# A decoder block with a Strassen-Winograd down projection: block sum T1 split under the up projection, sums S4 and T4 made ahead of their casts, results parked in dead activation blocks

## The chip, the cores and the metric

The kernel runs on one core of one Trainium2 chip. The metric is the device time of one launch in microseconds. The profile is of one execution, taken by the hardware profiler; its engines are TensorE (PE, with PEld for the weight loads that overlap the matmuls), VectorE (DVE), ScalarE (ACT), GpSimd (POOL) and SyncE (SP), whose queue issues nearly all DMAs here.

## The reference

One decoder layer on 512 tokens of width 1024, in float32:

```python
h   = rms_norm(x, norm_mix)
q, k, v, u = split(h @ w_in)                 # 4 x 512 columns
a   = moba_attention(q, k, v)                # 8 heads x 64, ALiBi, blocks of 256, causal
p   = multiscale_pool(u, w_pool, pool_scale) # 4 groups x 128
x   = x + concat(a, p) @ w_out
h   = rms_norm(x, norm_mlp)
x   = x + square(relu(h @ w_up)) @ w_down    # w_up 1024 x 4096, w_down 4096 x 1024
out = rms_norm(x, norm_final)
```

The change touches the last product alone: `square(relu(...)) @ w_down`.

## The kernel before

**Precision.** Each float32 operand is split in two float32r parts: `split_into` (line 147) has ScalarE cast the high part and VectorE subtract it from the source for the low part. A product is then three matmuls (`mm3`, line 195): high by high, high by low, low by high.

**Up projection.** `h @ w_up` is made transposed, in 32 blocks `f` of 128 hidden units by 512 tokens, 24 matmuls each. The loop of line 768 takes a block's weights from `ready`, has `sqrelu` make relu (ScalarE) and square (VectorE), and splits one further weight block (`prefetch`).

**Down projection.** Hidden blocks 0 to 27 form 14 pairs. Of each pair, the 2 x 2 blocks of activations (token halves by hidden blocks) and of w_down (hidden blocks by column halves) are multiplied in the Winograd form of Strassen's method, 7 products in place of 8. The blocks of activations and their sums lie in `a_p[p]`, six slots of 256 tokens; `a_sums` makes three of the sums. Of the weights three sums are needed: T1, T2, T3 are made by `t_sums` under the up projection and stored to scratch in DRAM (`t_store`): T2 and T1 in `t21`, T3 in `t3`. T4 is made in sweep 0 by one addition to a raw block (line 754); S4, the fourth sum of activations, is made by the subtraction of line 730. The products run in two sweeps over the pairs, since a core has eight banks:

- sweep 0 (line 809): per pair m1, m6, m7, m4, 24 matmuls of 512 columns. `a_split` splits four slots of the next pair's activations. Two `advance` calls split two blocks of weights for later.
- between the sweeps m1, m6, m7 are combined and leave their banks to `y` and `y2` (lines 816 to 828), which take the buffers of the normed activations (pool `hp`).
- sweep 1 (line 839): per pair m2, m5, m3, 18 matmuls. `a_split` first makes S4 of the next pair and then splits three slots. Two `advance` calls split T1 (512 columns, loaded as float32 from `t21`) and the pair's second block (1024 columns); at pairs 3, 5, 7, 9 of the list of steps (`LAST_AT`) a third splits a block of the tail. Two additions of finished blocks into `x` follow (`add_y`), eight in all.

Hidden blocks 28 to 31 are multiplied plainly in the tail (line 870), into the same banks, followed by the residual, the final norm and the stores.

**Order.** The program fixes each engine's order as it is written (`in_program_order`). Buffers set the rest: four raw blocks and four split ones in rotation, two of split activations (`ah`, `al`), which `t_load` uses under the up projection. SP issues the loads in program order too, and waits there for the buffer of each.

Of the kernel before, what the change touches and what calls it, by code (L numbers as in the profile page):

```python
# [50 lines left out]
def hybrid_block(  # L51
# [67 lines left out]
    for sweep, p, k in steps:  # L119
        if sweep == 2:  # L120
            parts = [(slice(None), rows(2 * PAIRS + p))]
        elif (sweep, k) == (0, 0):
            parts = [(LEFT, rows(2 * p, LEFT)), (RIGHT, t21[p][:, LEFT])]
        elif (sweep, k) == (0, 1):
            parts = [(LEFT, rows(2 * p + 1, LEFT)), (RIGHT, t3[p])]
# [546 lines left out]
    a_p = [ap.tile([P, 6, HT], F32, tag=f"a{p}", name=f"a{p}") for p in range(PAIRS)]
    tsum = {}

    def t_load(p):
        r0 = sp.tile([P, D], F32, tag="ah", name="r0", bufs=2)
        r1 = sp.tile([P, T], F32, tag="al", name="r1", bufs=2, padded_shape=[P, D])
        nc.sync.dma_start(r0, rows(2 * p))
        nc.sync.dma_start(r1, rows(2 * p + 1, RIGHT))
# [18 lines left out]
    def sqrelu(f, acc, ks=(0, 1)):  # L698
# [40 lines left out]
    def advance():
        sweep, p, k = steps.pop(0)  # L740
        raw, shape = raws.pop(0)
        if sweep == 2:
# [15 lines left out]
        if (sweep, k) == (0, 0):
            t2_of.append(raw[:, RIGHT])
        if k == 1 or sweep:  # L760
            load()
        if (sweep, k) == (0, 1):
            load()

    t2_of, w_pair = [], []
# [158 lines left out]
```

## Time and profile before

| | us |
|---|---|
| median of 3 runs (lowest, highest) | 541.66 (541.39, 542.94) |
| the profiled execution | 543.16 |
| its span, first to last instruction | 541.4 |
| TensorE busy, of the span | 520.1 |
| VectorE busy | 378.9 |
| ScalarE busy | 247.5 |

A busy TensorE is not one at its peak, since matmuls overlap: the records are 0.39 us long and begin 0.23 us apart. So the starts are what to read: the distance of two starts is the pace, and a larger one is a loss. In the profile, names without their numbers stand for all buffers of a kind: `whi` and `wlo` are split weights, `ah` and `al` split activations, `a` is a slot of `a_p`, `t` a scratch tensor, `r` the blocks of which the sums are made, `z` the relu, `yh` and `yl` the tiles `y` and `y2`, `wl_h` and `wl_l` the tail's weights.

### The profile page before, as it was taken

The page shows a single profiled execution, that of the slowest core. Times are in us where ns is not written, and L with a number is a line of the kernel's source. Part 1 is how long each engine was busy: PE and PEld are TensorE (multiplying, and loading weights), DVE is VectorE, ACT ScalarE, POOL GpSimd, SP SyncE. Part 2 cuts the span into 40 slices and gives each one's busy share as a digit, 9 for nine tenths or more (in the row PEclk, how much of TensorE's full clock was granted, in tenths as well). Part 3 has the DMA queues.
Part 4 walks back from the last instruction along what each step waited for, and adds up shares of the span by engine and source line. Part 5 has one row for each costly group of instructions (what it writes and reads, how often), then busy time and mean ns, then how long its engine had stood idle before and what let it go on. Part 6 is the DMA issues. An engine that isn't in the chain of part 4 may idle for free.

```text
span 541.4 us, 6738 instructions
## 1 busy us (share of the span) xinstructions
PE 520.1 (96%) x2411; PEld 427.7 (79%) x2411; DVE 378.9 (70%) x619; ACT 247.5 (46%) x415; POOL 56.0 (10%) x59
## 2 busy tenths in 40 slices
PE   8999999997999999999999999999999998899995
PEld 5888878886888898888888888887888875576784
DVE  4764898888968658655765576657878778767653
ACT  4534586876635433323232323245555545455233
POOL 2330351615300100000000000000000000000002
PEclk9999999999999999999999999999999999999999
DMA  8441240303234137867867878624555444556013
GB/s 281 146 116 41 69 125 11 123 6 117 78 117 119 37 93 234 276 228 245 300 215 251 270 240 259 227 77 157 199 195 205 163 169 157 185 184 213 2 40 117
DMA packets 72037, 85.14 MB, mean 157 GB/s; under 512 B 4033, under 2 KB 49601, under 8 KB 72002
## 3 DMA queue, kind: packets, MB, share of 16 engines
q1 hardware_dynamic: 71424, 83.64, 46.9%
q10 hardware_dynamic: 578, 1.05, 0.5%
q8 instruction: 19, 0.31, 0.2%
q14 instruction: 16, 0.13, 0.1%
HBM read 71.57 MB, written 13.11 MB: 156 GB/s over the span
## 4 chain that ended last, share of the span: by engine, by line
PE 77%; DVE 10%; ACT 6%; issue 5%; DMA 1%; POOL 0%; SPq 0%; POOLq 0%; DVEq 0%; ACTq 0%
PE bank L199 23%; PE bank L197 23%; PE bank L198 23%; PE bank L297 3%; PE bank L430 2%; ACT whi L148 1%; ACT ah L148 1%; PE bank L219 1%; DMA wvr<-in_w_in_dram 1%; DVE al L149 1%; PE bank L459 1%; DVE wlo L149 1%; DVE ptl L465 1%; DVE wl_l L149 1%; DVE p L436 1%
## 5 line engine op out<-in xcount | busy, mean ns | idle before, releaser
L197 PE MATMUL bank<-hh,whi 128*128 128x512 f32 (+1 forms) x376 | 141.7, 377 | 0.2 <-DVE qs L392 0.2
L199 PE MATMUL bank<-hh,wlo 128*128 128x512 f32 (+1 forms) x376 | 141.2, 376 | 0.0
L198 PE MATMUL bank<-hl,whi 128*128 128x512 f32 (+1 forms) x376 | 141.2, 376 | 0.0
L149 DVE TENSOR_TENSOR wlo<-raw,whi 128x1024 fp32r<-128x1024 f32 x101 | 116.5, 1161 | 33.5 <-ACT whi L148 32.7
L148 ACT CAST whi<-raw 128x1024 fp32r<-128x1024 f32 (+1 forms) x104 | 102.0, 994 | 37.6 <-DVE raw L754 29.3
L197 PE MATMUL bank<-whi,ah 128*128 128x512 f32 x196 | 77.9, 398 | 5.7 <-ACT ah L148 5.1
L197 PEld LDWEIGHTS bank<-hh,whi 128*128 128x128 f32 x376 | 70.8, 188 | 13.3 <-PE bank L459 0.4
L199 PEld LDWEIGHTS bank<-hh,wlo 128*128 128x128 f32 x376 | 70.8, 188 | 12.9
L199 PE MATMUL bank<-whi,al 128*128 128x512 f32 x196 | 78.1, 398 | 2.8 <-DVE al L149 2.7
L198 PEld LDWEIGHTS bank<-hl,whi 128*128 128x128 f32 x376 | 70.8, 188 | 12.5
L198 PE MATMUL bank<-wlo,ah 128*128 128x512 f32 x196 | 77.1, 394 | 0.0
L701 ACT ACTIVATE z<-bank 128x512 f32<-128x512 f32 (+1 forms) x35 | 19.7, 563 | 113.3 <-PE bank L199 107.2
L197 PEld LDWEIGHTS bank<-whi,ah 128*128 128x128 f32 x196 | 37.2, 190 | 16.8 <-ACT ah L148 8.4
L707 DVE TENSOR_TENSOR a<-bank,z 128x512 f32<-128x512 f32 (+1 forms) x31 | 19.8, 639 | 43.3 <-ACT z L701 43.3
L199 PEld LDWEIGHTS bank<-whi,al 128*128 128x128 f32 x196 | 37.2, 190 | 14.8 <-DVE al L149 7.2
L212 POOL TENSOR_TENSOR rstd<-ms,mhalf 128x1 f32<-128x1 f32 x12 | 6.6, 554 | 401.3 <-DVE ms L207 401.3
L198 PEld LDWEIGHTS bank<-wlo,ah 128*128 128x128 f32 x196 | 37.1, 189 | 7.5
L148 ACT CAST ah<-a 128x1024 fp32r<-128x1024 f32 (+1 forms) x28 | 26.3, 940 | 30.7 <-DVE a L730 30.7
L149 DVE TENSOR_TENSOR al<-a,ah 128x1024 fp32r<-128x1024 f32 (+1 forms) x28 | 30.5, 1088 | 13.4 <-ACT ah L148 13.4
L203 ACT ACTIVATE sq<-x 128x512 f32<-128x512 f32 (+2 forms) x17 | 10.3, 605 | 30.6 <-DVE x L865 17.1
L438 ACT ACTIVATE p<-p,mn 128x128 f32<-128x128 f32 (+3 forms) x32 | 18.0, 562 | 11.6 <-DVE rs L417 5.8
L418 DVE TENSOR_SCALAR p<-p,rs 128x128 f32<-128x128 f32 (+3 forms) x32 | 16.0, 501 | 1.1
(141 smaller groups left out, 696.9 us busy)
## 6 DMA issues: line engine op xcount, KB each, us to landing
raw<-in_w_up_dram SPq DMA_DIRECT2D x32, 512.0 KB, 5.5
raw<-t SPq DMA_DIRECT2D x42, 256.0 KB, 3.1
raw<-in_w_down_dram SPq DMA_DIRECT2D x18, 512.0 KB, 3.3
r<-in_w_down_dram SPq DMA_DIRECT2D x14, 512.0 KB, 3.3
t<-r SPq DMA_DIRECT2D x14, 512.0 KB, 6.2
raw<-in_w_down_dram SPq DMA_DIRECT2D x28, 256.0 KB, 2.6
raw<-in_w_in_dram SPq DMA_DIRECT2D x12, 512.0 KB, 3.8
raw<-in_w_out_dram SPq DMA_DIRECT2D x8, 512.0 KB, 3.3
```

The source lines that it names most:

```text
L148: nc.scalar.copy(hi, src)
L149: (sub or nc.vector).tensor_sub(lo, src, as32(hi))
L197: nc.tensor.matmul(acc, lhsT=a[0], rhs=b[0], start=first, stop=False)
L198: nc.tensor.matmul(acc, lhsT=a[0], rhs=b[1], start=False, stop=False)
L199: nc.tensor.matmul(acc, lhsT=a[1], rhs=b[0], start=False, stop=last)
L203: nc.scalar.activation(dump, src, AF.Square, scale=1.0 / 32, accum_out=ss[:, k:k + 1])
L297: nc.tensor.matmul(acc, lhsT=a, rhs=w, start=n == 0 and kd == 0, stop=n == 2 and kd == KD - 1)
L418: nc.vector.tensor_scalar_mul(p[:, :w], p[:, :w], rs)
L430: nc.tensor.matmul(by_qi[qi], lhsT=qs[:, tok(qi)], rhs=k[:, :w], start=n == 0, stop=n == 1)
L438: nc.scalar.activation(p[:, :w], p[:, :w], AF.Exp, scale=-1.0, bias=mn, accum_out=sm)
L701: nc.scalar.activation(z[:, :n * HT], acc, AF.Relu)
L707: nc.vector.tensor_mul(a_p[f // 2][:, at_slots, :], halves(acc), halves(z[:, :n * HT]))
```

## The change

- T1 is split in `t_sums`, under the up projection: ScalarE casts it into the free right half of `r1`, VectorE subtracts in place. `t_store` stores both tiles whole: T2 and T1's low part (`t2_t1l`), T3 and T1's high part (`t3_t1h`), 512 KB each. `t1_load` loads T1 split, for two pairs at once, into the `hp` buffers of the normed activations, in four requests of 256 KB; it is called after pairs 1, 3, 5, 7 of sweep 0 and pairs 1, 3, 5 of sweep 1.
- T4 is made by `t4` at the head of each pair of sweep 0, ahead of the casts; S4 by `s4`, two pairs ahead in sweep 1.
- Activation pairs 0 and 1 are both split under the last blocks of the up projection; the split of hidden block 31 moves to pair 1 of sweep 0.
- `y` lies in slots 4 and 5 of `a_p[7]` to `a_p[12]`, which sweep 1 does not read. `a_p` is made in two pools; the one of pairs 0 to 6 is closed at pair 5 of sweep 1 and its place holds the tail's weights (`wlh`, `wll`), which are split after steps 8, 10, 11, 13 now.

```diff
-LAST_AT = (3, 5, 7, 9)
+LAST_AT = (8, 10, 11, 13)
...
 for p in range(PAIRS):
-        steps += [(1, p, 0), (1, p, 1)]
+        steps.append((1, p, 1))
...
-    a_p = [ap.tile([P, 6, HT], F32, tag=f"a{p}", name=f"a{p}") for p in range(PAIRS)]
+    for half in (1, 0):
+        ap = pairs[half].enter_context(tc.tile_pool(name=f"ap{half}", bufs=1, reuse_waits="tile"))
...
     def t_sums(p):
         r0, r1 = tsum[p]
-        nc.vector.tensor_add(r1, r1, r0[:, RIGHT])
-        nc.vector.tensor_add(r0[:, RIGHT], r0[:, RIGHT], r0[:, LEFT])
-        nc.vector.tensor_add(r0[:, LEFT], r0[:, LEFT], r1)
+        (b11, b12), b22 = [as32(r0[:, cols]) for cols in HALF], as32(r1[:, LEFT])
+        nc.vector.tensor_add(b22, b22, b12)
+        nc.vector.tensor_add(b12, b12, b11)
+        nc.vector.tensor_add(b11, b11, b22)
+        split_into(r1[:, RIGHT], r0[:, RIGHT], b12)
 
     def t_store(p):
         r0, r1 = tsum.pop(p)
-        nc.sync.dma_start(t21[p], r0)
-        nc.sync.dma_start(t3[p], r1)
+        nc.sync.dma_start(t2_t1l[p], as32(r0))
+        nc.sync.dma_start(t3_t1h[p], as32(r1))
+    def t1_load(p):
+        tile_ = hp.tile([P, 2, 2, T], F32R, tag=f"h{'hl'[p // 2 % 2]}", name="t1")
+        for k in range(2):
+            nc.sync.dma_start(as32(tile_[:, k, 0, :]), t3_t1h[p + k][:, RIGHT])
+            nc.sync.dma_start(as32(tile_[:, k, 1, :]), t2_t1l[p + k][:, RIGHT])
+            t1[p + k] = tile_[:, k, 0, :], tile_[:, k, 1, :]
...
+            if f < NF - 1:
+                split_into(*late[-1], z)
...
+    def s4(p):
+        a = a_p[p]
+        nc.vector.tensor_sub(a[:, 1, :], a[:, 3, :], a[:, 1, :])
...
-            nc.vector.tensor_sub(a[:, 1, :], a[:, 3, :], a[:, 1, :])
             src = a[:, 1:4, :]
...
+    def t4():
+        r0, r1 = raws[0][0], raws[1][0]
+        nc.vector.tensor_add(r1[:, LEFT], r1[:, LEFT], r0[:, RIGHT])
...
-        if (sweep, k) == (0, 1):
-            nc.vector.tensor_add(raw[:, LEFT], raw[:, LEFT], t2_of.pop())
-        elif (sweep, k) == (1, 0):
-            cols = RIGHT
-        split_into(hi[:, cols], lo[:, cols], raw[:, cols])
+        split_into(hi, lo, raw)
+        load()
...
-        if f == NF - 2:
-            a_s.append(a_split(0, 0))
+        if f in (NF - 3, NF - 2):
+            a_s.append(a_split(len(a_s), 0))
...
+    y = [a_p[PAIRS // 2 + k][:, 4:6, :].rearrange("p s t -> p (s t)") for k in range(6)]
     for p in range(PAIRS):
         a, first, last = a_s.pop(0), p == 0, p == PAIRS - 1
-        a_s.append(a_split(p + 1, 0) if not last else a_split(0, 1))
+        if last:
+            s4(0)
+            a_s.append(a_split(0, 1))
+            s4(1)
+        else:
+            if steps[0][0] == 0:
+                t4()
+            if not first:
+                a_s.append(a_split(p + 1, 0))
...
         advance()
+        if p == 1:
+            split_into(*late[-1], z)
+        if p % 2 and p < 8:
+            t1_load(p - 1)
     for j in range(2):
-        nc.vector.tensor_sub(y2[:, j, :], y[:, 2 + j, :], m7[j])
+        nc.vector.tensor_sub(y[4 + j], y[2 + j], m7[j])
...
     for p in range(PAIRS):
         a, first, last = a_s.pop(0), p == 0, p == PAIRS - 1
+        if p + 2 < PAIRS:
+            s4(p + 2)
+        for _ in range(2 if 0 < p < 4 else 1):
+            if not first:
+                next(adds, None)
         if not last:
             a_s.append(a_split(p + 1, 1))
-        w0, w1 = ready.pop(0), ready.pop(0)
-        product(m2, a, 2, w1, LEFT, first, False)
-        product(m5, a, 1, w0, RIGHT, first, last)
-        product(m3, a, 0, w1, RIGHT, first, False)
-        for _ in range(2):
-            if steps:
-                advance()
-        if steps and steps[0][0] == 2:
+        w = ready.pop(0)
+        product(m2, a, 2, w, LEFT, first, False)
+        product(m5, a, 1, t1.pop(p), slice(None), first, last)
+        product(m3, a, 0, w, RIGHT, first, False)
+        while steps and (steps[0][0] == 2 or steps[0][1] <= p + 3):
             advance()
-        for _ in range(2):
-            next(adds, None)
+        if p % 2 and p + 7 < PAIRS:
+            t1_load(p + 7)
```

What stands on VectorE in two pairs of sweep 1, before (`a` is the sum S4, `al` and `wlo` are the low parts of activations and weights, `x` takes finished blocks in):

```order
L730 TENSOR_TENSOR a_2156<-a_2156 128x256
L149 TENSOR_TENSOR al<-a_2156,ah 128x768
L149 TENSOR_TENSOR wlo<-raw,whi 128x512
L149 TENSOR_TENSOR wlo<-raw,whi 128x1024
L149 TENSOR_TENSOR wl_l<-raw,wl_h 128x1024
L834 TENSOR_TENSOR x_105<-x_105,yl 128x512
L835 TENSOR_TENSOR x_105<-x_105,yl 128x512
L730 TENSOR_TENSOR a_2157<-a_2157 128x256
L149 TENSOR_TENSOR al<-a_2157,ah 128x768
L149 TENSOR_TENSOR wlo<-raw,whi 128x512
```

And the same engine in the same pairs now:

```order
L733 TENSOR_TENSOR a_2168<-a_2168 128x256
L852 TENSOR_TENSOR x_105<-x_105,a_2158 128x512
L853 TENSOR_TENSOR x_105<-x_105,a_2158 128x512
L145 TENSOR_TENSOR al<-a_2167,ah 128x768
L145 TENSOR_TENSOR wlo<-raw,whi 128x1024
L733 TENSOR_TENSOR a_2169<-a_2169 128x256
L850 TENSOR_TENSOR x_104<-x_104,a_2155 128x512
L851 TENSOR_TENSOR x_104<-x_104,a_2157 128x512
L145 TENSOR_TENSOR al<-a_2168,ah 128x768
L145 TENSOR_TENSOR wlo<-raw,whi 128x1024
```

Before, the sum and the low part behind it are of one pair; now the sum is one pair ahead, the additions stand between them, and the split of 512 columns is gone.

VectorE between the sweeps, before (`yh` and `yl` take the contents of the banks):

```order
L730 TENSOR_TENSOR a_2154<-a_2154 128x256
L149 TENSOR_TENSOR al<-a_2154,ah 128x768
L149 TENSOR_TENSOR wlo<-raw,whi 128x512
L822 TENSOR_TENSOR yh<-bank,yh 128x512 x2
L149 TENSOR_TENSOR wlo<-raw,whi 128x1024
L828 TENSOR_TENSOR yl<-yh,bank 128x512 x2
L730 TENSOR_TENSOR a_2155<-a_2155 128x256
L149 TENSOR_TENSOR al<-a_2155,ah 128x768
```

And now (the banks go to slots of `a_p`):

```order
L733 TENSOR_TENSOR a_2164<-a_2164 128x256
L145 TENSOR_TENSOR al<-a_2164,ah 128x768
L733 TENSOR_TENSOR a_2165<-a_2165 128x256
L145 TENSOR_TENSOR wlo<-raw,whi 128x1024
L836 TENSOR_TENSOR a_2156<-bank,a_2154 128x512
L836 TENSOR_TENSOR a_2157<-bank,a_2155 128x512
L145 TENSOR_TENSOR wlo<-raw,whi 128x1024
L846 TENSOR_TENSOR a_2158<-a_2156,bank 128x512
L846 TENSOR_TENSOR a_2159<-a_2157,bank 128x512
L733 TENSOR_TENSOR a_2166<-a_2166 128x256
L145 TENSOR_TENSOR al<-a_2165,ah 128x768
```

The split ahead of the first two subtractions has grown from 512 to 1024 columns, and a second sum stands ahead of it.

VectorE under the up projection, the sums of one pair, before:

```order
L149 TENSOR_TENSOR wlo<-raw,whi 128x1024
L716 TENSOR_TENSOR a_2166<-a_2166 128x256
L717 TENSOR_TENSOR a_2166<-a_2166 128x256
L718 TENSOR_TENSOR a_2166<-a_2166 128x256
L684 TENSOR_TENSOR r_3095<-r_3095,r_3094 128x512
L685 TENSOR_TENSOR r_3094<-r_3094 128x512
L686 TENSOR_TENSOR r_3094<-r_3094,r_3095 128x512
L707 TENSOR_TENSOR a_2167<-bank,z 128x2x256
```

And now (`rh` and `rl` are here the tiles `r0` and `r1`):

```order
L145 TENSOR_TENSOR wlo<-raw,whi 128x1024
L727 TENSOR_TENSOR a_2159<-a_2159 128x256
L728 TENSOR_TENSOR a_2159<-a_2159 128x256
L729 TENSOR_TENSOR a_2159<-a_2159 128x256
L683 TENSOR_TENSOR rl<-rl,rh 128x512
L684 TENSOR_TENSOR rh<-rh 128x512
L685 TENSOR_TENSOR rh<-rh,rl 128x512
L145 TENSOR_TENSOR rh<-rh,rl 128x512
L717 TENSOR_TENSOR a_2160<-bank,z 128x2x256
```

One subtraction of 512 columns has come in behind the three sums of weights.

## Rows read from the trace of the kernel before

**Rows 1.** Busy time in four stretches: up projection from its fourth block on, sweep 0, sweep 1, tail. Columns: stretch, then busy us and instructions of PE, PEld, DVE, ACT, POOL, then the granted TensorE clock, the DMA share and GB/s.

```profile
205.00:363.90 158.90, 158.90 (x707) 131.82 (x707) 104.44 (x149) 47.46 (x63) 0.00 (x0) 1.00 0.71 237
363.90:441.30 77.40, 76.69 (x337) 62.89 (x336) 56.85 (x59) 42.53 (x46) 0.00 (x0) 1.00 0.52 180
441.30:513.00 71.70, 63.86 (x254) 47.06 (x254) 53.62 (x71) 33.95 (x42) 0.00 (x0) 0.98 0.45 151
513.00:541.40 28.40, 22.26 (x109) 18.81 (x107) 13.21 (x26) 9.06 (x22) 4.51 (x7) 0.97 0.20 75
```

**Rows 2.** The waits of PE from 364 to 513 us, all of them: line, what ended the wait, us in total, times, longest.

```profile
PE bank L197 <- ACT ah L148: 5.1, 7, 1.4
PE bank L199 <- DVE al L149: 2.7, 9, 0.7
PE bank L197 <- DVE yl L828: 0.7, 1, 0.7
```

**Rows 3.** The timeline of ACT: the relu of two blocks of the up projection, one after the other. Columns: start, us, instruction, idle before it.

```profile
217.24 0.60 ACT L701 ACTIVATE z<-bank 128x512 f32<-128x512 f32 x1 [3.91 <-PE bank L199]
...
222.68 0.60 ACT L701 ACTIVATE z<-bank 128x512 f32<-128x512 f32 x1 [3.91 <-PE bank L199]
```

**Rows 4.** The timeline of PE: the first matmul of sweep 0, the one that waited in its second pair, the first of sweep 1, the first of the tail.

```profile
363.92 0.39 PE L197 MATMUL bank<-whi,ah 128*128 128x512 f32 x1
...
370.96 0.50 PE L199 MATMUL bank<-whi,al 128*128 128x512 f32 x1 [0.71 <-DVE al L149]
...
441.36 0.39 PE L197 MATMUL bank<-whi,ah 128*128 128x512 f32 x1
...
512.98 0.39 PE L197 MATMUL bank<-wl_h,rh 128*128 128x512 f32 x1
```

**Rows 5.** The timeline of DVE over one pair of sweep 1 (the two 512- and 1024-column splits are merged in one row).

```profile
450.58 0.42 DVE L730 TENSOR_TENSOR a<-a 128x256 f32<-128x256 f32 x1
451.95 0.96 DVE L149 TENSOR_TENSOR al<-a,ah 128x768 fp32r<-128x768 f32 x1 [0.95 <-ACT ah L148]
452.83 1.82 DVE L149 TENSOR_TENSOR wlo<-raw,whi 128x512 fp32r<-128x512 f32 x2
454.57 1.22 DVE L149 TENSOR_TENSOR wl_l<-raw,wl_h 128x1024 fp32r<-128x1024 f32 x1
455.70 0.68 DVE L834 TENSOR_TENSOR x<-x,yl 128x512 f32<-128x512 f32 x1
456.30 0.68 DVE L835 TENSOR_TENSOR x<-x,yl 128x512 f32<-128x512 f32 x1
456.91 0.42 DVE L730 TENSOR_TENSOR a<-a 128x256 f32<-128x256 f32 x1
```

**Rows 6.** The waits of all engines from 441 to 513 us, longest first, the first.

```profile
ACT ah L148 <- DVE a L730: 29.0, 13, 3.2
```

**Rows 7.** The timeline of ACT at the start of sweep 0: two casts of 1024 columns.

```profile
367.46 1.05 ACT L148 CAST whi<-raw 128x1024 fp32r<-128x1024 f32 x1 [1.36 <-DVE raw L754]
368.42 1.05 ACT L148 CAST ah<-a 128x1024 fp32r<-128x1024 f32 x1
```

**Rows 8.** The timeline of DVE between the sweeps.

```profile
441.86 1.28 DVE L822 TENSOR_TENSOR yh<-bank,yh 128x512 f32<-128x512 f32 x2
443.06 1.22 DVE L149 TENSOR_TENSOR wlo<-raw,whi 128x1024 fp32r<-128x1024 f32 x1
444.19 1.28 DVE L828 TENSOR_TENSOR yl<-yh,bank 128x512 f32<-128x512 f32 x2
```

**Rows 9.** The timeline of ACT between the sweeps.

```profile
438.89 0.83 ACT L148 CAST ah<-a 128x768 fp32r<-128x768 f32 x1 [1.68 <-DVE a L730]
439.63 1.07 ACT L818 COPY yh<-bank 128x512 f32<-128x512 f32 x2
440.59 0.63 ACT L148 CAST whi<-raw 128x512 fp32r<-128x512 f32 x1
```

**Rows 10.** Busy time in slices of sweep 1, columns as in rows 1; the clock is the third number from the end.

```profile
440.00:445.00 5.00, 4.34 (x20) 3.19 (x18) 4.47 (x7) 2.27 (x4) 0.00 (x0) 1.00 0.35 124
445.00:450.00 5.00, 4.55 (x18) 3.09 (x19) 4.05 (x7) 2.30 (x3) 0.00 (x0) 1.00 0.42 139
...
470.00:475.00 5.00, 4.74 (x13) 3.41 (x13) 3.78 (x5) 2.06 (x3) 0.00 (x0) 0.66 0.57 197
...
473.00:474.00 1.00, 1.00 (x4) 0.71 (x4) 0.23 (x1) 0.74 (x1) 0.00 (x0) 0.50 0.99 377
```

**Rows 11.** The timeline of SP's queue over one pair of the up projection: stores of the sums, the next pair's load, the loads behind it.

```profile
329.72 0.42 SPq L690 DMA_DIRECT2D t<-r  x1
...
334.44 0.33 SPq L678 DMA_DIRECT2D r<-in_w_down_dram  x1
...
335.94 0.42 SPq L144 DMA_DIRECT2D raw<-t  x1
339.75 0.33 SPq L144 DMA_DIRECT2D raw<-in_w_down_dram  x1
```

**Rows 12.** DMA issues from 205 to 360 us, the stores of the sums: count, KB each, median us from issue to landing.

```profile
t<-r SPq DMA_DIRECT2D x14, 512.0 KB, 6.2
...
t<-r SPq DMA_DIRECT2D x14, 256.0 KB, 5.5
```

**Rows 13.** The same from 365 to 510 us, the loads of the sums.

```profile
raw<-t SPq DMA_DIRECT2D x36, 256.0 KB, 3.1
```

More of the change, by code (lines that the diff above doesn't have):

```diff
@@ L106, in hybrid_block @@
     scr = ctx.enter_context(tc.tile_pool(name="scr", bufs=1, space=bass.MemoryType.DRAM))
-    t21 = [scr.tile([P, D], F32, tag=f"t21_{p}", name=f"t21_{p}") for p in range(PAIRS)]
-    t3 = [scr.tile([P, T], F32, tag=f"t3_{p}", name=f"t3_{p}") for p in range(PAIRS)]
+    t2_t1l = [scr.tile([P, D], F32, tag=f"ta{p}", name=f"ta{p}") for p in range(PAIRS)]
+    t3_t1h = [scr.tile([P, D], F32, tag=f"tb{p}", name=f"tb{p}") for p in range(PAIRS)]
     steps = [(0, p, k) for p in range(PAIRS) for k in range(2)]
     for p in range(PAIRS):
-        steps += [(1, p, 0), (1, p, 1)]
+        steps.append((1, p, 1))
         if p in LAST_AT:
@@ L121, in hybrid_block @@
             parts = [(slice(None), rows(2 * PAIRS + p))]
[L122 to L125, printed above, removed]
-        elif (sweep, k) == (1, 0):
-            parts = [(RIGHT, t21[p][:, RIGHT])]
+        elif sweep == 0:
+            parts = [(LEFT, rows(2 * p + k, LEFT)), (RIGHT, (t2_t1l, t3_t1h)[k][p][:, LEFT])]
         else:
@@ L667, in hybrid_block @@
     load()
-    pairs = ExitStack()
-    ap = pairs.enter_context(tc.tile_pool(name="ap", bufs=1, reuse_waits="tile"))
     HT = T // 2
-    a_p = [ap.tile([P, 6, HT], F32, tag=f"a{p}", name=f"a{p}") for p in range(PAIRS)]
+    pairs = [ExitStack(), ctx]
+    a_p = [None] * PAIRS
+    for half in (1, 0):
+        ap = pairs[half].enter_context(tc.tile_pool(name=f"ap{half}", bufs=1, reuse_waits="tile"))
+        for p in range(half * PAIRS // 2, (half + 1) * PAIRS // 2):
+            a_p[p] = ap.tile([P, 6, HT], F32, tag=f"a{p}", name=f"a{p}")
     tsum = {}
     def t_load(p):
[L676 to L679, printed above, removed]
+        r0, r1 = [sp.tile([P, D], F32R, tag=f"a{k}", name=f"r{k}", bufs=2) for k in "hl"]
+        nc.sync.dma_start(as32(r0), rows(2 * p))
+        nc.sync.dma_start(as32(r1[:, LEFT]), rows(2 * p + 1, RIGHT))
         tsum[p] = r0, r1
@@ L709, in sqrelu @@
             nc.vector.tensor_mul(z, acc, z)
-            r_s = [sp.tile([P, T], F32R, tag=f"r{k}", name=f"r{k}", bufs=LAST) for k in "hl"]
-            split_into(*r_s, z)
-            late.append(r_s)
+            late.append([sp.tile([P, T], F32R, tag=f"r{k}", name=f"r{k}", bufs=LAST) for k in "hl"])
+            if f < NF - 1:
+                split_into(*late[-1], z)
+        return z
     def a_sums(p):
@@ L742, in advance @@
         if sweep == 2:
-            if p % 2 == 0:
-                w_pair[:] = [hp.tile([P, 2, D], F32R, tag=f"h{k}", name=f"wl_{k}") for k in "hl"]
-            hi, lo = [v[:, p % 2, :] for v in w_pair]
+            hi, lo = [mp.tile([P, D], F32R, tag=f"wl{k}{p}", name=f"wl{k}{p}") for k in "hl"]
             w_last.append((hi, lo))
@@ L750, in advance @@
             ready.append((hi, lo))
-        cols = slice(None)
-        if (sweep, k) == (0, 1):
-            nc.vector.tensor_add(raw[:, LEFT], raw[:, LEFT], t2_of.pop())
-        elif (sweep, k) == (1, 0):
-            cols = RIGHT
-        split_into(hi[:, cols], lo[:, cols], raw[:, cols])
[L758 to L765, printed above, removed]
+        split_into(hi, lo, raw)
+        load()
     t_load(0)
@@ L778, in hybrid_block @@
             up(acc, ready.pop(0))
-            sqrelu(f, acc)
+            z = sqrelu(f, acc)
         if f < NF - 4:
@@ L782, in hybrid_block @@
         else:
+            if not odd:
+                t4()
             advance()
@@ L815, in hybrid_block @@
         if last:
-            y, y2 = [hp.tile([P, 4, T], F32, tag=f"h{k}", name=f"y{k}") for k in "hl"]
             for j in range(2):
-                nc.scalar.copy(y[:, j, :], m1[j])
+                nc.scalar.copy(y[j], m1[j])
         advance()
```

17 lines of the change are left out of this document (10 added, 7 removed).

## The prediction

> **What bounds the kernel now.** I read the windows first. In the up projection TensorE is busy for all 158.9 us while VectorE works 104.4 and ScalarE 47.5; in the stretch of the second sweep it is busy 63.9 of 71.7 us and VectorE 53.6 [rows 1]. The reader is to see that TensorE is the limit everywhere but there. The table of TensorE's waits says what ends them: `ah`, `al` and the combined block `yl`, all made by ScalarE and VectorE [rows 2].
>
> How much is lost? A full block of the up projection is 24 matmuls, and its `z` follows the one before by 222.68 - 217.24 = 5.44 us, so one matmul's pace is 0.2267 us [rows 3]. Between the first matmul of sweep 0 (363.92) and the first of the tail (512.98) lie 588 matmuls in 149.06 us [rows 4]. At pace they need 133.30. **15.76 us are lost**: 441.36 - 363.92 - 336 x 0.2267 = 1.27 in sweep 0, and 71.62 - 252 x 0.2267 = 14.49 in sweep 1. The waits of rows 2 sum to 8.5 only; the rest is slower first matmuls after waits and a stretch at a lower clock (rival A).
>
> Why sweep 1 loses: on VectorE one pair runs from the subtraction at 450.58 to the next at 456.91, 6.33 us, where TensorE's 18 matmuls need 4.08. In it VectorE stands still for 0.95 us (`al` waits for ScalarE's `ah`, which waits for the subtraction just made), splits T1 (0.60) and the second block (1.14), a block of the tail (1.13), and adds two finished blocks (0.60 each) [rows 5]. Over the stretch ScalarE waited 29.0 us for that subtraction [rows 6]: the two hand work to and fro, and nothing else is done in between.
>
> **The change, part by part.** (1) *Sweep 1, steady.* On VectorE I count 0.42 for 256 columns (busy time) and, from start to start, 0.88 for 768, 0.60 for 512 and 1.13 for 1024 [rows 5, 8]; a hand-over between engines adds 0.04 to 0.08, since 450.58 + 0.42 + a cast of 0.83 [rows 9] leaves 0.12 for two until `al` at 451.95. T1's split is gone from this stretch, S4 is made a pair and more ahead, so `ah` no longer waits for VectorE. A pair then costs VectorE 0.42 + 0.88 + 1.13 = 2.43 us; with two additions (pairs 1 to 3) 3.63; with a tail block (pairs 7, 8, 10) 3.56; with one of each (pair 5) 4.16. Only the last is over 4.08, by less than the pair before leaves free, and weight halves are made three pairs ahead. What stays as a chain: `ah` may start when TensorE leaves the buffer (two exist), so at a pair's start + 0.08; it takes 0.83, `al` 0.96: ready 1.9 us into a pair of 4.08. So steady sweep 1 runs at pace; its price is 252 x 0.2267 = 57.1 us.
>
> (2) *The hand-over between sweeps.* Four products leave their banks here, and VectorE is asked for more in a row than before: a whole 1024-column split stands ahead of each of the two groups of subtractions. I set the end of sweep 0 as E, and use ScalarE steps of 0.95 (1024), 0.74 (768) and 0.48 (bank copy) [rows 7, 9]. The last pair starts at E - 5.44. ScalarE: `whi` E - 5.36. VectorE: `wlo` E - 4.27, S4 E - 3.14. ScalarE: `ah` E - 2.64, copies E - 1.90 and E - 1.42, `whi` E - 0.94 to E + 0.11. VectorE: `wlo` E + 0.15, then the first y subtraction E + 1.28 to E + 1.97. TensorE wants that bank after six matmuls, E + 1.36, and gets it at E + 2.02: **0.66 lost**, and 0.11 since the first matmul after a wait is 0.50 long, not 0.39 [rows 4]. Next `wlo` E + 2.48 and the m7 subtraction E + 3.61 to E + 4.29; TensorE wants its bank at E + 3.49 and gets it at E + 4.34: **0.85 + 0.11**. After that `al` of pair 1 ends at E + 6.2 and is wanted, as third operand, at E + 6.3. Together 1.73 us. In before the same place cost 0.7 [rows 2], with shorter splits ahead. If the copies and casts are some tenths quicker the sum falls towards 1; it cannot go below 0.
>
> (3) *Start of sweep 0.* TensorE waited there for `al` at 370.96 [rows 4]: ScalarE's casts for pair 1 came at 367.46 and 368.42 [rows 7], behind the relu and the split of the last block. Now the first two activation pairs are split under the up projection, and the last block's split is put off to pair 1. I take the 1.27 us back in full. In the pairs after, VectorE has 0.60 + 3 x 1.14 = 4.02 us of work in 5.44, as before.
>
> (4) *Up projection.* Each of 14 pairs gains a 512-column cast and subtraction, 0.69 us on VectorE and 0.62 on ScalarE: 9.7 onto 104.4 and 8.7 onto 47.5 of 158.9 us [rows 1]. The subtraction waits for the cast, and the cast stands ahead of the next block's relu on ScalarE, so this relu comes some 0.5 us late; who waits is the bank, and eight rotate. Nought, covered by the idle third of VectorE; without cover it would be 14 x 1.3 = 18 us. The stores grow by 256 KB a pair: 14 x 0.262 MB / 158.9 us = 23 GB/s onto 237. SP's queue holds its next load of w_down until a store has landed; it issued the store at 329.72, the load at 334.44, was done with the pair's loads at 336.36 and then waited for VectorE until 339.75 [rows 11]: 3.4 us of cover. A 512 KB store lands in 6.2 us, a 256 KB one behind it in 5.5 [rows 12], so I take the larger one as 0.7 later, and the cost as nought.
>
> The Trainium skill (DMA: Bandwidth & Descriptors, Anatomy of one DMA) says, of transfers that GpSimd issues (here SP does), that most of the fixed cost is the wait for the receipt of the last byte, and that it is longest when the target is HBM. That speaks against storing more; the rows agree, since a 256 KB store took 5.5 us where a 256 KB read of the same scratch took 3.1 [rows 12, 13]. By the page the larger store adds little; by the row, 0.7; the sum is the same.
>
> (5) *Loads of T1.* Four requests of 1 MB each fall into sweep 0 (pairs 1, 3, 5, 7), three into sweep 1, each asked for some seven pairs ahead. In sweep 1 they stand on SP behind TensorE's release of a T1 buffer, and later loads behind them; these are four raw blocks ahead. Sweep 0 moves 180 GB/s where the up projection moved 237 [rows 1]. I take nought; a raw block is freed 2.4 us into a pair (cast and subtraction), its two parts land 0.4 + 3.1 us later [rows 13], at 0.5 into the next pair, and T4 wants it 2.4 into that one: 1.9 us of cover, and 1.6 more before an `al` made behind T4 is late. So it may land some 3 us later before TensorE sees it.
>
> **Sum.** 15.76 - 1.73 = 14.0 us back; the tail has the same matmuls. The profiled execution took 543.16 us (span 541.4), 1.5 over the median of 541.66. Against its own time: 529.2. If those 1.5 us lie in what is kept, the median becomes 527.7; if they lie in the low-clock stretch that goes, 529.2. I take **528.6**.
>
> **Rivals.** *A, more waits at the hand-over, and the clock.* Late in sweep 1, behind pair after pair of waits, TensorE's granted clock fell to 0.50, that is 1.2 GHz, at 473; the slice 470 to 475 shows 0.66, so 5 x 0.34 = 1.7 us lost. Between 440 and 450, where it began 38 matmuls in place of 44, it stayed at 1.00, 2.4 GHz [rows 10]. The hand-over is no thinner than that. The Trainium skill (TensorE: Matmul & The Clock Gate, Part 1) says that the clock is gated by how busy TensorE has been of late and is half when it isn't. By that page alone a fall here is possible. Price: 1.7 and as much again of waits, 532. Against it: 440 to 450.
> *B, T1 loads delay sweep 0.* One request of 1 MB takes 4.4 to 5.8 us at the rates of rows 1. If a raw block waited out all of it, 1.4 to 2.8 us pass the 3 us of cover, four times: 6 to 11 us, 535 to 540. Against it: the raw blocks are asked for ahead of T1 in the same queue.
> *C, slower than before: the up projection becomes bound by SP's queue.* If the two stores landed more than 3.4 us later than now, every pair would be longer by the excess; 13 x 1.0 eats the gain, so from 4.4 us on the kernel is slower, at 5 us about 549. Against it: the expected 0.7, and a DMA share of 0.71 that grows to 0.78.
>
> **How the numbers follow.** Forecast (526.5 to 531): 0.75. A (531 to 533.5): 0.10. B: 0.07. C: 0.05, and 0.03 for what I don't see, between 533 and no change. A measurement can tell about 0.3%, 1.6 us, from no change. Faster: 0.75 + 0.10 + 0.07 + some of the last, 0.93; same 0.02; slower 0.05. The lower end is the loss taken back whole, 541.66 - 15.76 = 525.9, nearly; the upper takes in A: 526.3 to 533.5.
>
> **What would show it.** Sweep 1 from its first to its last matmul near 59 us (71.6 now), with two waits of 0.6 to 0.9 us on the y subtractions and nearly none on `ah` and `al`; no wait at the start of sweep 0, which takes 76.2; the up projection without a wait and its `z` still 5.44 apart; the clock at 1.00 through both sweeps; ScalarE's wait for the S4 line gone. Wrong would be: waits of VectorE or ScalarE for raw blocks in sweep 0 (B), `z` more than 5.44 apart (C), or `al` still late in the steady pairs, which breaks (1).

## The result, and the profile after

| | us |
|---|---|
| after, median of 4 runs (lowest, highest) | 529.62 (529.42, 529.92) |
| before, median of 4 runs (lowest, highest) | 542.3 (541.39, 544.0) |
| after / before | 0.9763, 95% interval 0.9736 to 0.979 |
| the profiled execution after, its span | 529.51, 527.7 |

The windows of the kernel after, with the columns of [rows 1]. The first two stretches are cut at the same times as there, the other two where sweep 1 now ends:

```profile
205.00:363.90 158.90, 158.90 (x708) 131.89 (x708) 114.35 (x165) 55.69 (x79) 0.00 (x0) 1.00 0.79 260
363.90:441.30 77.40, 77.40 (x343) 64.15 (x342) 57.12 (x58) 44.40 (x46) 0.00 (x0) 1.00 0.71 245
441.30:500.00 58.70, 57.34 (x252) 46.77 (x251) 44.17 (x57) 24.39 (x28) 0.00 (x0) 1.00 0.46 161
500.00:528.00 28.00, 21.58 (x106) 18.24 (x104) 12.54 (x25) 9.04 (x22) 4.51 (x7) 0.97 0.20 76
```

Most of the gain is in the third stretch: 58.7 us where it was 71.7. VectorE's 53.62 us there fell to 44.17, and what it lost there it has more of in the first (104.44 to 114.35), where TensorE is still busy throughout. How long each sweep really takes is read from the starts, which follow.

The timeline of PE after, the starts that answer to [rows 4]: first of sweep 0, first of sweep 1, the two that waited with the one ahead of the first of them, first of the tail.

```profile
364.04 0.39 PE L193 MATMUL bank<-whi,ah 128*128 128x512 f32 x1
...
440.20 0.39 PE L193 MATMUL bank<-whi,ah 128*128 128x512 f32 x1
...
441.33 0.39 PE L195 MATMUL bank<-whi,al 128*128 128x512 f32 x1
442.41 0.50 PE L193 MATMUL bank<-t,ah 128*128 128x512 f32 x1 [0.69 <-DVE a L836]
...
444.73 0.50 PE L193 MATMUL bank<-whi,ah 128*128 128x512 f32 x1 [0.67 <-DVE a L846]
...
499.30 0.39 PE L193 MATMUL bank<-wlh,rh 128*128 128x512 f32 x1
```

From 364.04 to 499.30 are 135.26 us for the same 588 matmuls, 149.06 before: 13.80 came back. Sweep 0 takes 76.16, its bare pace, where it took 77.44; sweep 1 takes 59.10, 1.97 over pace, where it took 71.62. Some 1.5 of the 13.80 are the low-clock stretch of [rows 10], in which eight matmuls started about 0.43 apart. The two waits in the fence are all that PE has between 364 and 500 us; the 16 waits on `ah` and `al` of [rows 2] are gone. Set against the profiled execution of before: 543.16 - 13.80 = 529.36, plus 0.12 of a later start of sweep 0, against 529.51 measured. So, between these two executions, the sweeps are the whole of it.

The timeline of DVE over a steady pair of sweep 1 after, to set beside [rows 5]:

```profile
457.40 0.42 DVE L733 TENSOR_TENSOR a<-a 128x256 f32<-128x256 f32 x1
457.73 0.69 DVE L852 TENSOR_TENSOR x<-x,a 128x512 f32<-128x512 f32 x1
459.38 0.96 DVE L145 TENSOR_TENSOR al<-a,ah 128x768 fp32r<-128x768 f32 x1 [0.96 <-ACT ah L144]
460.34 1.23 DVE L145 TENSOR_TENSOR wlo<-raw,whi 128x1024 fp32r<-128x1024 f32 x1
461.48 0.42 DVE L733 TENSOR_TENSOR a<-a 128x256 f32<-128x256 f32 x1
```

S4 to S4 is 4.08 us, TensorE's pace for 18 matmuls; it was 6.33, in a pair that had a second addition, a tail block and T1's split as well. VectorE still stands idle for 0.96 us in front of `al`, but now that is slack. Who it waits for is seen in the waits of ACT from 441 to 500 us, which were led by VectorE's S4 in [rows 6]:

```profile
ACT ah L144 <- issue: 17.8, 9, 2.3
ACT ah L144 <- PE bank L194: 8.4, 3, 4.0
```

`ah` is now late because TensorE has not yet left its buffer: three of the waits name it. The other nine name nothing ("issue"), but there too the casts of `ah` start 4.08 us apart, at TensorE's pace. An idle engine waiting for the bottleneck costs nothing; the same 0.95 us before was a wait in a ring that TensorE had to sit out.

### The profile page after: what moved, and what is told of

Same layout as the page of the kernel before. It is cut to its first block, busy times and chain, and to the rows that moved or that the text cites. A ratio compares the mean times of both kernels' runs of the same rounds, so it can differ in the third digit from the quotient of the medians.

```text
span 527.7 us, 6731 instructions
## 1 busy us (share of the span) xinstructions
PE 514.7 (98%) x2411; PEld 429.4 (81%) x2411; DVE 378.9 (72%) x619; ACT 247.8 (47%) x415; POOL 56.0 (11%) x59
## 4 chain that ended last, share of the span: by engine, by line
PE 88%; DVE 6%; ACT 2%; issue 2%; DMA 1%; POOL 0%; SPq 0%; POOLq 0%
PE bank L193 26%; PE bank L195 26%; PE bank L194 26%; PE bank L293 5%; PE bank L426 2%; PE bank L215 1%; DMA wvr<-in_w_in_dram 1%; PE bank L455 1%; DVE ptl L461 1%; DVE p L432 1%; ACT whi L144 1%; DVE wlo L145 1%; DVE ka L398 1%; DVE mx L508 0%; PE bank L473 0%
## 5 line engine op out<-in xcount | busy, mean ns | idle before, releaser
L145 DVE TENSOR_TENSOR wlo<-raw,whi 128x1024 fp32r<-128x1024 f32 x87 | 107.5, 1238 | 27.5 <-ACT whi L144 25.4
L144 ACT CAST whi<-raw 128x1024 fp32r<-128x1024 f32 x90 | 94.1, 1054 | 31.1 <-PE bank L195 23.5
L194 PEld LDWEIGHTS bank<-hl,whi 128*128 128x128 f32 x376 | 70.8, 188 | 12.7
L193 PE MATMUL bank<-whi,ah 128*128 128x512 f32 x168 | 65.5, 390 | 0.7 <-DVE a L846 0.7
L194 PE MATMUL bank<-wlo,ah 128*128 128x512 f32 x168 | 65.4, 390 | 0.0
L195 PE MATMUL bank<-whi,al 128*128 128x512 f32 x168 | 65.4, 390 | 0.0
L193 PEld LDWEIGHTS bank<-whi,ah 128*128 128x128 f32 x168 | 31.5, 188 | 7.6 <-DVE a L846 1.1
L194 PEld LDWEIGHTS bank<-wlo,ah 128*128 128x128 f32 x168 | 31.6, 188 | 6.5
L195 PEld LDWEIGHTS bank<-whi,al 128*128 128x128 f32 x168 | 31.6, 188 | 6.5
L144 ACT CAST rl<-rh 128x512 fp32r<-128x512 f32 x14 | 8.7, 622 | 57.6 <-DVE rh L684 57.6
```

The costliest lines, as they stand in the source:

```text
L144: nc.scalar.copy(hi, src)
L145: (sub or nc.vector).tensor_sub(lo, src, as32(hi))
L193: nc.tensor.matmul(acc, lhsT=a[0], rhs=b[0], start=first, stop=False)
L194: nc.tensor.matmul(acc, lhsT=a[0], rhs=b[1], start=False, stop=False)
L195: nc.tensor.matmul(acc, lhsT=a[1], rhs=b[0], start=False, stop=last)
```

## Experiments

**Theory.** Sweep 1 ran at VectorE's time for a pair, which was work plus standing still for `ah`; the change takes both below 4.08 us, and what is left is the hand-over between the sweeps. **Rivals.** Only one of the two parts does it, S4 ahead or T1 split early. Or the loss came from loads, which the change has moved as well: then more bytes in the up projection or in sweep 0 would show it at once.

**After again, beside other runs.**

> The changed kernel once more, beside the two below on one chip: 529.6 us by every theory.

530.23 us (528.65 to 530.86), ratio 0.9766, 0.9747 to 0.9784. The sweeps took 135.26 us again, to the hundredth; only the start of sweep 0 lay elsewhere, at 364.74. In what follows the sweeps' stretch, first matmul of sweep 0 to first of the tail, is therefore read beside the median: it was the same in both executions of after, while the time moved.

**S4 late again, all else as after.**

```diff
         else:
+            s4(p)
             src = a[:, 1:4, :]
...
-            s4(0)
             a_s.append(a_split(0, 1))
-            s4(1)
...
-        if p + 2 < PAIRS:
-            s4(p + 2)
```

> S4 is again made right ahead of its own cast, T1 stays split under the up projection. My theory (VectorE's time per pair, work and standing still together, against TensorE's 4.08 us): a pair costs VectorE 0.42 + 0.95 + 0.88 + 1.13 = 3.38 us, 4.58 with two additions and 4.51 with a tail block, so only pairs 1 to 3 lose, 0.5 us each: about 531 us, 1.5 over the changed kernel. Rival 1 (the to and fro between ScalarE and VectorE was the whole loss, T1's split nothing): the 12.4 us for which VectorE stood still come back, 541. Rival 2 (only the moved T1 counts): 529.6, no change.

531.58 us (530.93 to 532.5), ratio 0.9785, 0.9767 to 0.9804. Sweeps 138.05: 2.8 more than after, where 1.5 was forecast, and 11.0 less than before. Of these 11.0, 1.3 are the start of sweep 0, which this kernel has as after has it. Sweep 1 alone took 61.89, from its first matmul to the first of the tail:

```profile
439.29 0.39 PE L193 MATMUL bank<-whi,ah 128*128 128x512 f32 x1
...
501.18 0.39 PE L193 MATMUL bank<-wlh,rh 128*128 128x512 f32 x1
```

The timeline of DVE of this kernel, a pair with two additions:

```profile
447.74 0.42 DVE L733 TENSOR_TENSOR a<-a 128x256 f32<-128x256 f32 x1
449.14 0.96 DVE L145 TENSOR_TENSOR al<-a,ah 128x768 fp32r<-128x768 f32 x1 [0.98 <-ACT ah L144]
...
452.44 0.41 DVE L733 TENSOR_TENSOR a<-a 128x256 f32<-128x256 f32 x1
```

The pair is 4.70 us: work of 3.7 and the old idle 0.98 between sum and low part. Pairs without an addition or a tail block fit into 4.08 even so.

**S4 ahead in the kernel before, T1 still split in sweep 1.** The edit is made in before:

```diff
+    def s4(p):
+        a = a_p[p]
+        nc.vector.tensor_sub(a[:, 1, :], a[:, 3, :], a[:, 1, :])
...
-            nc.vector.tensor_sub(a[:, 1, :], a[:, 3, :], a[:, 1, :])
             src = a[:, 1:4, :]
...
+        if last:
+            s4(0)
         a_s.append(a_split(p + 1, 0) if not last else a_split(0, 1))
+        if last:
+            s4(1)
...
+        if p + 2 < PAIRS:
+            s4(p + 2)
```

> The kernel before with one part of the change alone: S4 is made two pairs ahead; T1 is still split in sweep 1, the rest is as before. My theory: a pair costs VectorE 0.42 + 0.88 + 0.60 + 1.13 + 1.20 = 4.23 us with additions and 5.36 with a tail block too, pairs 0 to 3 lose 2.9 us together, the start of sweep 0 keeps its 1.3 and the hand-over its 0.8: about 533 us. Rival 1 (the to and fro was the whole loss): about 530. Rival 2 (only the moved T1 counts): no gain on the kernel before, 541 to 543.

535.35 us (534.19 to 537.67), ratio 0.9868, 0.984 to 0.9896. Sweeps 140.25, 8.8 less than before, all of it in sweep 1, which took 62.80; the gain was put too high. The same two starts:

```profile
441.19 0.39 PE L197 MATMUL bank<-whi,ah 128*128 128x512 f32 x1
...
503.99 0.39 PE L197 MATMUL bank<-wl_h,rh 128*128 128x512 f32 x1
```

The longest of the two waits of PE that are left (the other is 0.6 us at the hand-over), and then the timeline of DVE over a pair with two additions and a tail block:

```profile
PE bank L199 <- DVE al L149: 3.8, 6, 1.4
```

```profile
449.94 0.42 DVE L722 TENSOR_TENSOR a<-a 128x256 f32<-128x256 f32 x1
450.27 0.95 DVE L149 TENSOR_TENSOR al<-a,ah 128x768 fp32r<-128x768 f32 x1
...
455.22 0.42 DVE L722 TENSOR_TENSOR a<-a 128x256 f32<-128x256 f32 x1
```

No standing still, and yet 5.28 us: there is more work than 4.08 in such a pair. In sweep 1 the two parts of the change give 9.7 and 8.8 us alone and 12.5 together. Neither rival that names one part holds: either part takes most of the loss away, and the last 2.8 to 3.7 us need both. (The S4-late kernel also has the tail's splits and the additions in their new places; how much of the 9.7 us that gives was not tried by itself. And neither of the two kernels has the low-clock stretch of before in its sweeps, so its 1.5 us are in both numbers.)

**The hand-over.** In the last pair of sweep 0 both weight splits move behind the two groups of subtractions:

```diff
-        advance()
         if last:
...
                 nc.vector.tensor_sub(y[2 + j], m6[j], y[j])
+        else:
+            advance()
...
-        advance()
+        if not last:
+            advance()
...
         nc.vector.tensor_sub(y[4 + j], y[2 + j], m7[j])
+    advance()
+    advance()
```

> The changed kernel with the order turned round in the last pair of sweep 0: the banks are combined ahead of the two splits of weights, which come behind. My theory: the two waits of 0.7 us on the y subtractions and the slow matmuls behind them were all that sweep 1 lost (59.10 us against 57.13), so 527.6 to 528.0 us. Rival (the wait only moves, to al of pair 1 or to the weights of pair 2): 529 to 530, with a wait named so.

528.69 us (528.2 to 530.5), ratio 0.9737, 0.9714 to 0.976. Both waits on the banks are gone, and one on `al` of pair 1 has come, since the two splits now stand ahead of it on VectorE. That is the rival: the wait has in part moved. The only wait of PE between the sweeps:

```profile
PE bank L195 <- DVE al L145: 0.9, 1, 0.9
```

The sweeps take 134.50, 0.76 less than after; the intervals of the two ratios overlap. The next step follows from that row: the sum S4 of pair 2 and the split of activation pair 1 go ahead of the two weight splits as well. The first two pieces of the edit above stay; the rest now reads, against after:

```diff
         nc.vector.tensor_sub(y[4 + j], y[2 + j], m7[j])
+    s4(2)
+    a_s.append(a_split(1, 1))
+    advance()
+    advance()
...
-        if p + 2 < PAIRS:
+        if not first and p + 2 < PAIRS:
...
-        if not last:
+        if not (first or last):
             a_s.append(a_split(p + 1, 1))
```

> The changed kernel with the banks combined, and then the sum S4 of pair 2 and the split of activation pair 1, ahead of the two splits of weights. In the run before, with the first of these alone, the two waits on the y subtractions went and one on al of 0.9 us came. My theory: al of pair 1 is now ready 1.9 us into sweep 1, the weights 4.2 us in and wanted at 8.2, so no wait is left in either sweep: sweep 1 takes 57.2 us, the whole 1.9 us less than the changed kernel, 527.7. Rival (something else is late next, the weights of pair 2 or the sums): 528.5 to 529.5.

527.85 us (527.16 to 528.71), ratio 0.9727, 0.9711 to 0.9743; after, on the same chip, 530.23. The windows of its two sweeps:

```profile
363.70:439.90 76.20, 76.20 (x338) 63.09 (x337) 56.69 (x58) 42.68 (x44) 0.00 (x0) 1.00 0.75 249
439.90:497.00 57.10, 57.10 (x253) 47.30 (x252) 43.61 (x56) 26.07 (x29) 0.00 (x0) 1.00 0.50 166
```

PE is busy for all of both. 133.28 us for 588 matmuls is bare pace (133.30), with no wait left: the hand-over was all that after still lost in its sweeps. This version beats both kernels: its interval ends below the start of that of after on the same chip (0.9747).

**The start of sweep 0 as before.** One activation pair split under the up projection, not two, and the last block's split back in its place:

```diff
-            if f < NF - 1:
-                split_into(*late[-1], z)
+            split_into(*late[-1], z)
...
-        if f in (NF - 3, NF - 2):
+        if f == NF - 2:
             a_s.append(a_split(len(a_s), 0))
...
-            if not first:
-                a_s.append(a_split(p + 1, 0))
+            a_s.append(a_split(p + 1, 0))
...
-        if p == 1:
-            split_into(*late[-1], z)
```

> The changed kernel with the start of sweep 0 undone: the second activation pair is split in pair 0 of sweep 0 and hidden block 31 in its old place. My theory: TensorE waits again for al in the second pair, 1.1 to 1.3 us, 530.8 us. Rival (the additions made ahead of the casts alone have removed that wait): no change, 529.6.

530.69 us (530.26 to 531.06), ratio 0.9768, 0.9752 to 0.9784. Sweeps 135.68: the edit is worth 0.4 us of the 1.27 that the start cost before. The median lies at the forecast 530.8 by luck, since a wait of 1.1 to 1.3 us was forecast and by the starts 0.3 came. The timeline of ACT, where [rows 7] had an idle 1.36 us for T4's addition:

```profile
366.74 1.05 ACT L144 CAST whi<-raw 128x1024 fp32r<-128x1024 f32 x1
367.69 1.04 ACT L144 CAST ah<-a 128x1024 fp32r<-128x1024 f32 x1
```

The cast follows without a wait, since T4 is added ahead of the casts in this kernel as in after. Most of what the prediction gave to the early splits goes, by this, to T4's place. That is argued from the two timelines; T4's place was not tried alone.

**More bytes stored in the up projection.** Rival C is put to the test: each pair stores 512 KB more, and in a second kernel 1 MB more, to scratch that nothing reads.

```diff
         nc.sync.dma_start(t3_t1h[p], as32(r1))
+        nc.sync.dma_start(more_t[p], as32(r1))
```

> The changed kernel with one more store of 512 KB a pair under the up projection (r1 is stored a second time, to a tensor that nothing reads). My theory: the cover of SP's queue still holds, z stays 5.44 us apart, 529.6 to 531 us. Rival C of the prediction (each us by which the stores land beyond 3.4 costs every pair that us): the third store adds 512 KB / 240 GB/s = 2.2 us to a landing that has already grown from 6.2 to 7.3, still about within the cover; 530 to 540 if it is not.

529.96 us (528.92 to 531.41), ratio 0.9771, 0.9746 to 0.9796: nothing that shows (the sweeps take 135.27), at a DMA share of 0.88 and 302 GB/s over the up projection. VectorE now waits for the second block of its sums and the less for the relu behind it (16.7 us in all, 30.7 in after), and TensorE has no wait. The row of the first in the waits of DVE:

```profile
DVE rl L684 <- DMA rl<-in_w_down_dram: 20.0, 11, 3.1
```

The second kernel:

```diff
         nc.sync.dma_start(t3_t1h[p], as32(r1))
+        nc.sync.dma_start(more_t[2 * p], as32(r1))
+        nc.sync.dma_start(more_t[2 * p + 1], as32(r0))
```

> The changed kernel with 1 MB more stored a pair under the up projection (both tiles a second time, to a tensor that nothing reads): 2.83 + 1.05 = 3.88 MB a pair, 357 GB/s at the present pace, as much as the best slices of the trace moved. My theory of the cover: it ends here; the stores land some 4 us later, 0.6 to 2 us beyond the cover, of which 13 pairs pay 8 to 26 us, less what is split ahead: 533 to 550, z more than 5.44 apart. Rival (the up projection has more slack than SP's wait shows): no change, 529.6.

565.02 us (564.25 to 567.45), ratio 1.0426, 1.04 to 1.0452. Here the cover is gone, and it costs more than was supposed (533 to 550). The timeline of SP's queue over one pair:

```profile
322.76 0.33 SPq L677 DMA_DIRECT2D rh<-in_w_down_dram  x1
...
324.73 3.14 SPq L691 DMA_DIRECT2D ta<-rh  x1
...
329.27 1.22 SPq L694 DMA_DIRECT2D tc<-rh  x1
336.58 0.33 SPq L677 DMA_DIRECT2D rh<-in_w_down_dram  x1
```

Load to load is 13.8 us, where two blocks of TensorE take 10.9; 6.1 of it SP stands still until the last store has landed and the tile may be loaded again. Yet on the mean the DMA engines moved less than with half the extra bytes, 281 GB/s at a share of 0.80. Within the pair they are full at first (0.99 and 323 GB/s from 324.7 to 330.5) and less so while SP stands still (0.74 from 330.5 to 336.5). So the closed ring of load, sums, stores and landing on one queue leaves them partly idle; how much of the 13.8 us is the ring and how much their rate, this run does not tell apart. Sweep 0 starts at 393.42, 29.4 us later than after; the sweeps behind it take 140.84. The waits of PE from 205 to 394 us, the two longest:

```profile
PE bank L194 <- ACT whi L145: 9.0, 6, 2.7
PE bank L194 <- ACT ah L145: 8.7, 1, 8.7
```

With 2.1 more for `wlo` they are 19.8 of the 29.4 us. For much of the rest the clock fell, as rival A has it in another place: the granted clock from 205 to 393.4 us was 0.95, and in after's up projection it was 1.00.

**Loads of T1, rival B.** First each of them is issued twice, into the same tile (the second brings the same data):

```diff
             nc.sync.dma_start(as32(tile_[:, k, 1, :]), t2_t1l[p + k][:, RIGHT])
+            nc.sync.dma_start(as32(tile_[:, k, 0, :]), t3_t1h[p + k][:, RIGHT])
+            nc.sync.dma_start(as32(tile_[:, k, 1, :]), t2_t1l[p + k][:, RIGHT])
```

> The changed kernel with each T1 load requested twice (the same bytes into the same tile), so 7 MB more are read in the two sweeps. My theory: raw blocks may land 3 us later before TensorE sees it, so no change, 529.6 us, VectorE waiting for raw blocks at most. Rival B of the prediction (the T1 loads are near to delaying sweep 0): 535 to 540.

578.34 us (577.67 to 580.96), ratio 1.0673, 1.0645 to 1.0701. This is no measure of bytes. The waits of SP:

```profile
SPq L701 <- DMA t<-tb: 53.9, 14, 6.9
```

The second load of a tile waits at SP for the first to land, and the raw blocks behind it aren't asked for until then. The run shows the price of a queue that stands still for some 4 us twice in each of the seven calls, and of the clock that falls behind such waits (0.91 over the sweeps, 36.1 us of listed waits of PE), not that of its traffic. Hence another kernel, which adds 512 KB to each pair's load as a copy from w_down to scratch that nothing reads:

```diff
             nc.sync.dma_start(as32(tile_[:, k, 1, :]), t2_t1l[p + k][:, RIGHT])
+            nc.sync.dma_start(more_t[p + k], rows(2 * (p + k)))
```

> The changed kernel in which each T1 load is followed by a copy of 512 KB in DRAM, from w_down to a tensor that nothing reads, so two such copies stand behind the loads of two pairs; no request waits for another's landing, as the doubled loads of the run before did. My theory (in that run SP stood still between the requests, 40.3 us, and it was this and not the bytes that cost 49 us): 529.6 to 532 us. Rival B (the bytes themselves delay raw blocks): 535 or more, with VectorE waiting for raw blocks in sweep 0.

534.37 us (533.1 to 535.46), ratio 0.9845, 0.9827 to 0.9864. Sweeps 140.76, 5.5 over after and all of it in sweep 0. That is more than the 529.6 to 532 forecast, and nearer to the rival. The waits of DVE for loads in it, and those of PE that follow:

```profile
DVE raw L755 <- DMA raw<-in_w_down_dram: 10.8, 4, 3.6
```

```profile
PE bank L196 <- DVE al L146: 4.3, 3, 2.0
```

The first of them in the timelines of DVE and PE:

```profile
392.55 0.69 DVE L755 TENSOR_TENSOR raw<-raw 128x512 f32<-128x512 f32 x1 [3.63 <-DMA raw<-in_w_down_dram]
...
394.44 0.50 PE L196 MATMUL bank<-whi,al 128*128 128x512 f32 x1 [2.01 <-DVE al L146]
```

Between 365 and 500 us the 256 KB blocks of w_down land 6.0 us after their issue (the median), in after 3.4. Behind each of the four calls in sweep 0 T4's addition is held up (3.63, 1.95, 3.53 and 1.67 us), and by the starts each reaches TensorE through `al`, 1.46 us shorter (2.18, 0.49, 2.07 and 0.21, and 0.11 behind each). So rival B's mechanism exists. The prediction's 1.6 us of cover behind T4 measured 1.46; its 1.9 ahead of T4 was not measured by itself. In after, no wait in the sweeps is put down to a load.

## Why the prediction was right, and where a term was off

**Steady sweep 1, (1): right.** Forecast bare pace; the pair measured 4.08, and outside the hand-over's 1.9 us the whole sweep lost 0.07. S4's experiment shows that the slack is real: with S4 late a pair has 4.70.

**The hand-over, (2): right in place and size.** Forecast waits of 0.66 and 0.85 us with 0.11 behind each, 1.73 in all. From start to start the two matmuls came 0.85 and 0.83 us late (442.41 - 441.33 less one pace of 0.23 is the first), and 0.11 more behind each: 1.90. The timeline of DVE there, beside [rows 8]:

```profile
440.53 1.23 DVE L145 TENSOR_TENSOR wlo<-raw,whi 128x1024 fp32r<-128x1024 f32 x1 [0.63 <-ACT whi L144]
441.67 1.28 DVE L836 TENSOR_TENSOR a<-bank,a 128x512 f32<-128x512 f32 x2
442.87 1.22 DVE L145 TENSOR_TENSOR wlo<-raw,whi 128x1024 fp32r<-128x1024 f32 x1
444.00 1.28 DVE L846 TENSOR_TENSOR a<-a,bank 128x512 f32<-128x512 f32 x2
```

With E at 440.20, the subtractions were forecast for E + 1.28 and E + 3.61; they started at E + 1.47 and E + 3.80. The order was read rightly, and its remedy took the whole 1.97 us out.

**The start of sweep 0, (3): right in size, wrong in cause.** All 1.27 us came back. But of the early splits only 0.4 comes. The rest stood, as far as the timelines show, in the row that was read past: ScalarE's idle 1.36 us for the addition at the old T4 line [rows 7], which the change makes ahead of the casts. The full size was luck: another part of the same change brought what the named one did not.

**The up projection, (4): right in the result, wrong in the cover.** No wait, and sweep 0 starts 0.12 us from where it did. The stores' landings after, to set beside [rows 12]:

```profile
ta<-rh SPq DMA_DIRECT2D x14, 512.0 KB, 7.3
tb<-rl SPq DMA_DIRECT2D x14, 512.0 KB, 6.6
```

Both land 1.1 us later than before (6.2 and 5.5), where 0.7 was supposed. The first did so without a byte more, and with 512 KB more again the two landed in 6.7 and 6.4, so it isn't the size of the store alone. What SP pays for it is in its waits for stores from 205 to 364 us, after and then before:

```profile
SPq L676 <- DMA ta<-rh: 59.7, 12, 6.5
...
SPq L677 <- DMA tb<-rl: 10.5, 12, 0.9
```

```profile
SPq L678 <- DMA t<-r: 56.1, 12, 6.5
...
SPq L679 <- DMA t<-r: 4.7, 12, 1.7
```

70.2 us against 60.8, 0.8 a pair. But the cover of 3.4 was read from one late pair [rows 11]. The longest row of SP's waits for VectorE from 225 to 330 us, before and then after:

```profile
SPq L144 <- DVE wlo L149: 11.6, 7, 3.4
```

```profile
SPq L140 <- DVE a L717: 0.9, 2, 0.5
```

In all these waits were 12.2 us over nearly ten pairs, 1.3 a pair, and in after they are 0.9: this cover was used up there. That nothing was lost, with 512 KB more either, shows a further cover behind it: VectorE's spare time in a block, of which that run drew up to 3.1 us. The rule of the Trainium skill that was weighed here (DMA: Bandwidth & Descriptors, Anatomy of one DMA), by which most of the fixed cost is the wait for the receipt, is neither borne out nor refuted by these rows, since a landing holds the wait behind other requests too. The prediction's 5.5 us for a store against 3.1 for a read don't bear it out either: that store stands behind one of 512 KB, and in after 256 KB reads of scratch took 6.9 and 7.5 us (medians, 205 to 360 us).

**T1's loads, (5): right.** No wait in the sweeps is put down to a load. Of the bound of 3 us the extra copies measured the part behind T4, 1.46 where 1.6 stood.

**The total.** The sum said 14.0 us, and 13.80 came back; it gave 529.2 against the profiled execution, which measured 529.51. The step that went the wrong way by 1.0 us is the last: half of the 1.5 us between the profiled execution and the median was put into what is kept. The low-clock stretch of [rows 10] is gone in after, as the windows of the same slices show (the first holds the hand-over).

```profile
440.00:445.00 5.00, 3.64 (x15) 2.42 (x14) 4.47 (x6) 2.22 (x3) 0.00 (x0) 1.00 0.30 105
...
470.00:475.00 5.00, 5.00 (x23) 4.14 (x23) 3.43 (x5) 2.90 (x4) 0.00 (x0) 1.00 0.89 308
```

By medians the gain is 12.7 us (542.3 to 529.62), near the 12.5 that the reckoning against the profiled execution gives (541.66 to 529.2). That makes it the likelier one, but it isn't settled: before itself ran from 541.38 to 544.11 over all its runs here, and which of them have a low-clock stretch stays open.

**The rivals.** A didn't come: 13 matmuls began between 440 and 445, where pace gives 22, and the clock stayed at 1.00, 2.4 GHz. (The windows count 15, since they take in what began earlier; by starts the 38 of the prediction, from 440 to 450, are 35, and after has 35 there too.) B and C are real mechanisms that this change stays short of; C's price, once reached, was 2.9 us in the pair shown for the second 512 KB, the fallen clock included.

## What to carry to other kernels

Where two engines hand work to and fro inside a pair, count the time of one pair on the slower of them, idle time included, against the pace of the bottleneck: making an input a pair ahead removes the idle part, moving a split elsewhere removes the work, and the two overlap (9.7 and 8.8 us alone, 12.5 together in sweep 1). After such a change look at the place where stages meet, and put there whatever frees a bank ahead of whatever only feeds a later pair; then ask which product the displaced work was for. Loads and stores that look free are so by a cover of a few us on a queue, which can be read from its gaps over many pairs, not from one, and it ends sharply: 512 KB more per pair cost nothing that shows, 1 MB cost 35 us.

## What the hardware showed unasked

- A second load into a tile that is still being loaded held the whole queue in this program: SP stood still for 53.9 us in 14 waits at that line, and the kernel lost 48.7 us (578.34 against 529.62), for 7 MB of loads.
- A queue in a ring of loads and stores can keep the mean below the rate that the DMA engines reach: 281 GB/s at 1 MB extra per pair, where 512 KB extra ran at 302 without loss. The long issue of the first store on SP, 3.14 us in the pair shown, is no mark of the slower one: in after it took from 0.34 to 3.27.
- The landing of a 256 KB load of w_down went from 3.4 us (median, 209 GB/s between 365 and 500 us in after) to 6.0 with the copies, at 267. Whether the traffic does it or the copies ahead on the same queue was not told apart.
